# Splitting the branch weights beside the router's product, and reading their halves back from memory

## The chip, the cores and the metric

The kernel runs on one core of a Trainium2 chip. The metric is the device time of one execution in microseconds (us). Five engines matter: PE (TensorE, with PEld for its weight loads), DVE (VectorE), ACT (ScalarE), POOL (GpSimd) and SP (SyncE), which issues most transfers in one queue, in order.

## The reference

One decoder layer on 1024 tokens of width 1024, in float32. What bears on the change:

```python
u = x @ w_in                                   # projections for both mixers
y_a = dilated_mixer(a_qkv)                     # 256 wide
y_b = nsa_mixer(b_q, b_kv, b_gate, ...)        # 512 wide
merged = g_a * (y_a @ w_branch_a) + g_b * (y_b @ w_branch_b)
mix = merged @ w_out
h = layer_norm(ALPHA * x + mix, ln1_g, ln1_b)
ffn = hier_moe(h, w_coarse, ..., w_gate_up, w_down)   # router, then 2 of 32 experts
```

`w_branch_a` is 256x1024 and `w_branch_b` 512x1024: together six blocks of 128x1024.

## The kernel before, in words

Float32 products are made of three products of halves. A tile is split into a high part (a rounding copy on ACT) and a low part (the tile less its high part, on DVE or POOL): `split`, lines 120 to 125. A 128x1024 page is 512 KB.

The stages in order of time: the projections with the dilated attention; a stretch with the compression of keys and values and the router's product (up to about 475 us); the sparse attention for two groups (to about 850 us); the branch products, the gates, the output product; the experts.

PE's order is written out by hand through the attention. The projections are a stream of jobs, `stream` (line 222), of which `chunk()` gives PE six matmuls at a time between other work; their raw weights come through `wload` (line 212) and are split by `wsplit`. The other engines and SP take their order from a planner: among what is ready in its own simulated time, the instruction earliest in the program goes first. Tiles of one tag share a fixed number of pages; a page goes to the next asker when all accesses to its last tile are done. Each engine then runs its list strictly in order.

The router's product (`router`, line 750) forms w_out times the router's weights in eight steps. Each step loads one raw page `wo` of tag `t` (four pages), splits it into `woh` and `wol` in tags `th` and `tl` (two pages each, line 628), one step ahead of the product, and yields; the caller runs `for _ in wo_: chunk()` (line 818), so that projections stand between the steps. After steps 3 and 7 the sum is turned through two more pages of tag `t`, `oU` and `oT`. The compression before it uses the same three tags. `t_close()` (line 821) ends them, and the sparse attention's pages take their ground.

The six blocks of branch weights are handled in `open_branches` (line 976), called in the middle of the second group's attention, when the last projection is done and its memory is free: each block comes into one of two raw pages, ACT makes its high part, POOL its low part (`WLO` is 6), into the tag `w` of 20 pages. Right after them four blocks `y` of the branches' input go through the same two raw pages (`yload`, line 966), with the low parts on POOL too (`YLO` is 4). From that call on, what the attention issues has a raised priority in the planner. Two more blocks of `y` follow when the attention has ended, in halves, second half first; the branch products start with the second half of the tokens.

Of the kernel before, what the change touches and what calls it, by code (L numbers as in the profile page):

```python
# [9 lines left out]
FP = mybir.dt.float32  # L10
FR = mybir.dt.float32r
# [49 lines left out]
WLO = 6  # L61
# [16 lines left out]
def tile_hybrid(ctx: ExitStack, tc: tile.TileContext, x, xT, w_t, w_gate, pos_k, w1_k, w2_k, pos_v, w1_v, w2_v,  # L78
                w_a, w_b, w_out, w_oT, ln1_g, ln1_b, w_r, b_r, w_gu, w_dn, ln2_g, ln2_b, out, dbg=None):
    nc = tc.nc  # L80
    dbg = dbg or {}

    def pool(name, side, **kw):
        st = ExitStack()
        p = st.enter_context(tc.tile_pool(name=name, bufs=1, side=side, reuse_waits="tile", **kw))
        return p, st.close

    def pages(pl, tag, n):
        def f(name, dt=FP, shape=(128, 1024)):
            return pl.tile(list(shape), dt, name=name, tag=tag, bufs=n)  # L90
        return f

    def slots(pl, tag, n):

        def slot(i):
            return lambda name, dt=FP, shape=(128, 1024): pl.tile(list(shape), dt, name=name, tag=f"{tag}{i}", bufs=1)
        return [slot(i) for i in range(n)]
# [17 lines left out]
    dram = ctx.enter_context(tc.tile_pool(name="dram", bufs=1, space=DRAM))  # L115
# [4 lines left out]
    def split(raw, ph, pl, name, eng=None):  # L120
        hi = ph(name + "h", FR)
        lo = pl(name + "l", FR)
        nc.scalar.copy(hi, raw)  # L123
        (eng or nc.vector).tensor_tensor(lo, raw, hi.bitcast(FP), op=OP.subtract)  # L124
        return hi, lo
# [3 lines left out]
    def bank(tag):  # L129
        p, n, _ = ps_cur[0]  # L130
        tag = alias.get(tag, tag)
        return p.tile([128, 512], FP, name=tag, tag=tag, bufs=n[tag])
# [8 lines left out]
    def masked(pl, t, lo=None, keep=True):  # L141
        n = t.shape[1]
        m = pl("mk", FP, (128, n))
        nc.vector.tensor_scalar(m, t, 0.0, NEG, op0=OP.is_gt, op1=OP.mult)
        if lo is not None:
            m2 = pl("mk2", FP, (128, n))
            nc.vector.tensor_scalar(m2, t, lo, NEG, op0=OP.is_lt, op1=OP.mult)
            nc.vector.tensor_tensor(m, m, m2, op=OP.add)
        if keep:
            nc.vector.tensor_tensor(t, t, m, op=OP.add)  # L150
        else:
            nc.vector.tensor_copy(t, m)
# [22 lines left out]
    for k in range(8):  # L175
        r = s_pool.tile([128, 1024], FP, name=f"xr{k}")
# [67 lines left out]
    def chunk(n=1):  # L244
        for _ in range(n):
            clock[0] += 1
            next(strm, None)
            for d in [d for d in later if d[0] <= clock[0]]:
                later.remove(d)
                d[1]()  # L250
# [268 lines left out]
    def nsa_jobs(d):  # L519
        G = d["G"]  # L520
        k = (24 + 2 * G, nk_sink(d))
        v = (25 + 2 * G, v_sink(1, d["vt"], d["V"], lambda *a: nv(*a), 2))
        q = [(18 + 2 * G + p, lazy(lambda Q, p=p: q_sink(Q, d["sc"][p], 1), lambda: nq("nq", FR), 2, d["Q"][p]))
             for p in range(2)]
        return k, v, q
# [10 lines left out]
    k, v, q = nsa_jobs(N[0])  # L536
    jobs += [(22, c_sink("k")), k, (23, c_sink("v")), v, *q]
    jobs += fill[MG0:MG0 + MG1]
    k, v, q = nsa_jobs(N[1])
# [25 lines left out]
    for g in range(3):  # L565
# [3 lines left out]
        t = c_pool.tile([100, 512], FR, name=f"rw{g}")  # L569
# [58 lines left out]
    tpage, thpage, tlpage = pages(t_pool, "t", 4), pages(t_pool, "th", 2), pages(t_pool, "tl", 2)  # L628
# [121 lines left out]
    def router():  # L750
        def load(i):
            half, q = i // 4, i % 4
            r = tpage("wo", FP, (128, 2, 512))
            nc.sync.dma_start(r, w_oT[q * 256:q * 256 + 256, half * 512:half * 512 + 512].rearrange(
                "(a p) c -> p a c", p=128))
            hi, lo = thpage("woh", FR, (128, 2, 512)), tlpage("wol", FR, (128, 2, 512))
            nc.scalar.copy(hi, r)
            nc.vector.tensor_tensor(lo, r, hi.bitcast(FP), op=OP.subtract)
            return hi, lo
        ts = [load(0)]  # L760
        for i in range(8):
            if i < 7:
                ts.append(load(i + 1))
            half, q = i // 4, i % 4
            if q == 0:
                ps = bank("av")
            for j in range(2):
                for t in ts[i]:
                    nc.tensor.matmul(ps, wgd[:, 2 * q + j], t[:, j], start=q == 0 and j == 0 and t is ts[i][0],
                                     stop=q == 3 and j == 1 and t is ts[i][1])  # L770
            yield
            if q == 3:
                gT, gU = tpage("oT", FP, (64, 512)), tpage("oU", FP, (64, 512))
                nc.scalar.copy(gU, ps[64:128])
                nc.vector.tensor_tensor(gT, ps[0:64], gU, op=OP.add)
                yield
                ps = bank("pt")
                for b in range(4):
                    nc.tensor.transpose(ps[:, b * 64:b * 64 + 64], gT[:, b * 128:b * 128 + 128], ident[0:64, 0:64])
                nc.vector.tensor_copy(oW[:, 4 * half:4 * half + 4],  # L780
                                      ps[:, 0:256].rearrange("p (b c) -> p b c", b=4)[:, :, 0:36])

    wo_ = router()
    next(ck)
    chunk(3)
    for _ in range(3):
# [29 lines left out]
    masked(tpage, DW, -511.0)  # L816
    masked(tpage, MC, keep=False)
    for _ in wo_:
        chunk()
    chunk(done + 48 - clock[0])  # L820
    t_close()
# [142 lines left out]
    Y, W = [], []  # L964

    def yload(k, pgs, cut):
        hi, lo = pgs("yh", FR), pgs("yl", FR)
        for i in reversed(range(cut)):
            c = slice(i * 1024 // cut, (i + 1) * 1024 // cut)
            r = raw2("yr")  # L970
            nc.sync.dma_start(r[:, c], yad[k, :, c] if k < 2 else ybd[k - 2, :, c])
            nc.scalar.copy(hi[:, c], r[:, c])
            (nc.gpsimd if k < YLO else nc.vector).tensor_tensor(lo[:, c], r[:, c], hi[:, c].bitcast(FP), op=OP.subtract)
        Y.append((hi, lo))

    def open_branches():
        nonlocal rc_pool, rc_close, raw_pool, raw_close, raws, raw2, b_pool, b_close, bpage
        mg_close()
        w_close()
        x_close()  # L980
        rc_pool, rc_close = pool("rconst", "left")
        raw_pool, raw_close = pool("raw", "left")
        raws = slots(raw_pool, "r", NRAW)
        turns = itertools.cycle(raws)
        raw2 = lambda *a: next(turns)(*a)
        b_pool, b_close = pool("br", "left")
        bpage = pages(b_pool, "w", 20)
        for k in range(6):
            r = raw2("wab")
            nc.sync.dma_start(r, w_a[k * 128:k * 128 + 128, :] if k < 2 else w_b[(k - 2) * 128:(k - 1) * 128, :])  # L990
            W.append(split(r, bpage, bpage, "wab", nc.gpsimd if k < WLO else None))
        for k in range(4):
            yload(k, bpage, 1)

# [9 lines left out]
    for G in range(2):  # L1004
# [25 lines left out]
        for i, (n, p) in enumerate(us):  # L1030
            nxt = full(i + 2) if i + 2 < len(us) else iter(())
            grp = nsa_ta(d, n, p, P.pop(i))
            pieces = 0
            if i + 2 < len(us):
                m = us[i + 2][0]
                pieces = 2 * ((3 if m == 7 else 1 if 64 + (m + 1) * 128 <= 512 else 2) + (2 if m > 3 else 1))
            given = 0
            for gi, (tr, mul) in enumerate(grp):
                tr()
                step(mul)  # L1040
                want = pieces * (gi + 1) // len(grp)
                while given < want:
                    next(nxt, None)
                    given += 1
                    drip(0)
                drip(1)
                if G == 0 and i + 2 >= len(us):
                    chunk(2)
            for _ in nxt:
                pass  # L1050
            if G and b_pool is None and clock[0] >= end:
                open_branches()
                last_ = tc.high_priority(PRIO)
                last_.__enter__()
# [92 lines left out]
    for half in (1, 0):  # L1147
        if not half:
            mt_take(0)
        for j in range(NBR if half else 0, 8):  # L1150
# [4 lines left out]
            if (half, j) in WOJ:  # L1155
                k = WOJ.index((half, j))
# [851 lines left out]
```

## Time and profile before

| | us |
|---|---|
| median of 3 runs | 1684.24 |
| the runs | 1683.39 to 1689.32 |
| the profiled execution | 1687.2 |
| its span in the profile | 1685.3 |

The profile shows one execution: the busy time of each engine, what each waited for, and what the transfers did. Its own time is 1.9 us above its span and 3.0 us above the median of the runs.

### The profile page before, as it was taken

What the parts mean: (1) busy time and instruction counts of PE and PEld (TensorE: products, weight loads), DVE (VectorE), ACT (ScalarE), POOL (GpSimd) and SP (SyncE); (2) the same over time, 40 slices, a digit from 0 to 9 for tenths busy, and PEclk for the clock granted to TensorE, in tenths of its full rate; (3) what the DMA queues carried; (4) which work ended last, traced back from release to release, by engine and by line L of the source; (5) the groups of instructions that cost most, each with busy time, mean ns of one, the idle gap of its engine ahead of it and who ended that gap; (6) DMA issues with size and microseconds to landing.
All of it is one profiled execution on the core that took longest, in us unless ns stands there. A gap on an engine that the chain in (4) does not pass through costs nothing. (4 is left out here: it accounts for less than half of the span.)

```text
span 1685.3 us, 24695 instructions
## 1 busy us (share of the span) xinstructions
PE 1583.9 (94%) x8105; PEld 1305.3 (77%) x8105; DVE 1241.6 (74%) x2716; ACT 1113.4 (66%) x2046; POOL 469.6 (28%) x416
## 2 busy tenths in 40 slices
PE   7999999999999999999799996999999999999992
PEld 6888888777778987788678895777777777777771
DVE  5555553257867774588877797898888998989994
ACT  5566666526567785578933013778898888889882
POOL 1011113341222332323610152133431331233132
PEclk9999999999999999999999997999999999999996
DMA  7111111243420111001255767999999999999982
GB/s 267 46 38 38 39 38 63 75 110 89 148 73 31 49 34 34 25 18 52 89 206 182 297 218 255 337 342 341 368 361 356 340 346 360 366 348 358 370 281 58
DMA packets 115395, 313.87 MB, mean 186 GB/s; under 512 B 30061, under 2 KB 34285, under 8 KB 115265
## 3 DMA queue, kind: packets, MB, share of 16 engines
q1 hardware_dynamic: 101968, 287.23, 47.0%
q0 software_dynamic: 13296, 25.05, 6.0%
q8 instruction: 65, 1.06, 0.3%
q14 instruction: 66, 0.53, 0.1%
HBM read 290.04 MB, written 46.98 MB: 200 GB/s over the span
## 5 line engine op out<-in xcount | busy, mean ns | idle before, releaser
L1507 DVE TENSOR_TENSOR el<-er,eh 128x1024 fp32r<-128x1024 f32 x384 | 448.7, 1219 | 36.6 <-ACT eh L1506 34.8
L1506 ACT CAST eh<-er 128x1024 fp32r<-128x1024 f32 x384 | 391.5, 1056 | 46.8 <-PE pt L1524 33.2
L233 PE MATMUL pp<-xh,wh 128*128 128x512 f32 x672 | 271.6, 404 | 1.6 <-DVE q L288 1.6
L235 PE MATMUL pp<-xh,wl 128*128 128x512 f32 x672 | 264.7, 394 | 0.0
L234 PE MATMUL pp<-xl,wh 128*128 128x512 f32 x672 | 263.0, 391 | 0.0
L1524 PE MATMUL av<-eh,xt 128*128 128x512 f32 x512 | 196.7, 394 | 1.4 <-ACT xt L1493 1.2
L1524 PE MATMUL pt<-eh,xt 128*128 128x512 f32 x512 | 197.3, 395 | 0.0
L1550 POOL DMA_INDIRECT ybuf<-y,idx x30 | 103.3, 3444 | 172.0 <-ACT y L1549 151.0
L235 PEld LDWEIGHTS pp<-xh,wl 128*128 128x128 f32 x672 | 126.4, 188 | 29.3
L233 PEld LDWEIGHTS pp<-xh,wh 128*128 128x128 f32 x672 | 126.5, 188 | 20.8 <-DVE q L288 2.0
L1524 PE MATMUL sc<-eh,at 128*128 128x512 f32 x512 | 142.3, 399 | 0.0
L234 PEld LDWEIGHTS pp<-xl,wh 128*128 128x128 f32 x672 | 126.8, 189 | 19.2
L898 POOL TENSOR_TENSOR pw<-pw,st 128x64 f32<-128x64 f32 (+5 forms) x128 | 85.6, 698 | 185.8 <-DVE st L893 152.8
L1524 PEld LDWEIGHTS av<-eh,xt 128*128 128x128 f32 x512 | 96.8, 189 | 24.8 <-ACT xt L1493 1.6
L1524 PEld LDWEIGHTS pt<-eh,xt 128*128 128x128 f32 x512 | 96.8, 189 | 22.8
L936 DVE TENSOR_TENSOR PT<-pt,PT 128x512 fp32r<-128x512 f32 (+1 forms) x136 | 90.9, 671 | 25.8 <-ACT PT L935 24.1
L1524 PEld LDWEIGHTS sc<-eh,at 128*128 128x128 f32 x512 | 93.3, 188 | 20.7 <-ACT eh L1506 0.8
L1524 PE MATMUL av<-el,xt 128*128 128x512 f32 x256 | 106.4, 416 | 3.0 <-DVE el L1507 2.4
L1524 PE MATMUL pt<-el,xt 128*128 128x512 f32 x256 | 101.2, 396 | 0.0
L124 POOL TENSOR_TENSOR wl<-wr,wh 128x1024 fp32r<-128x1024 f32 x24 | 57.6, 2402 | 135.0 <-ACT wh L123 129.2
L935 ACT CAST PT<-pt 128x512 fp32r<-128x512 f32 (+1 forms) x136 | 76.7, 567 | 17.7 <-PE pt L928 15.9
L1401 POOL DMA_INDIRECT xg<-hbuf,idx x31 | 33.5, 1080 | 193.2 <-PE pp L1487 183.3
(447 smaller groups left out, 3600.6 us busy)
## 6 DMA issues: line engine op xcount, KB each, us to landing
er<-in_w_gu_dram SPq DMA_DIRECT2D x256, 512.0 KB
er<-in_w_dn_dram SPq DMA_DIRECT2D x128, 512.0 KB
wr<-in_w_t_dram SPq DMA_DIRECT2D x44, 512.0 KB
mgd<-mg SPq DMA_DIRECT2D x32, 256.0 KB
G<-mgd SPq DMA_DIRECT2D x32, 256.0 KB
xr<-in_xT_dram SPq DMA_DIRECT2D x8, 512.0 KB
out_dram<-in_ln_b_dram SPq DMA_DIRECT2D x8, 512.0 KB
wo<-in_w_oT_dram SPq DMA_DIRECT2D x8, 512.0 KB
```

The lines of the kernel that those rows point to most:

```text
L124: (eng or nc.vector).tensor_tensor(lo, raw, hi.bitcast(FP), op=OP.subtract)
L233: nc.tensor.matmul(ps, wh[:, kk], xh[k][:, c], start=k == 0, stop=False)
L234: nc.tensor.matmul(ps, wh[:, kk], xl[k][:, c], start=False, stop=False)
L235: nc.tensor.matmul(ps, wl[:, kk], xh[k][:, c], start=False, stop=k == 7)
L898: nc.gpsimd.tensor_tensor(t, t, st[:, 1, hi_, i:i + 1].to_broadcast([128, w]), op=OP.mult)
L935: nc.scalar.copy(t[:, 0], src)
L936: nc.vector.tensor_tensor(t[:, 1], src, t[:, 0].bitcast(FP), op=OP.subtract)
L1401: nc.gpsimd.indirect_dma_start(out=t, out_offset=None, in_=hbuf, in_offset=bass.IndirectOffsetOnAxis(ap=ids, axis=0), bounds_check=S - 1, ...
L1506: nc.scalar.copy(wh, r)
L1507: nc.vector.tensor_tensor(wl, r, wh.bitcast(FP), op=OP.subtract)
L1524: nc.tensor.matmul(pss[h], a[j == 1][:, kk], (wl if j == 2 else wh)[:, h], start=o == 0 and j == 0, stop=o == n - 1 and j == 2)
L1550: s_ = nc.gpsimd.indirect_dma_start(out=ybuf, out_offset=bass.IndirectOffsetOnAxis(ap=self.ids, axis=0), in_=y, in_offset=None, bounds_che ...
```

## The change

The six blocks are loaded and split earlier, in a generator that is stepped once after each `chunk()` of the router's loop. It uses the tags of the router: raw page `t`, high part `th`, low part `tl`, with the low part on DVE (no engine is named). Both parts are written to a new buffer in device memory, `wabd`, 12 pages of 512 KB. In `open_branches` the 12 parts are read straight into their pages; the six loads, copies and subtractions there are gone.

```diff
-    wo_ = router()
+    wabd = dram.tile([6, 2, 128, 1024], FP, name="wabd")
+
+    def branch_weights():
+        def load(k):
+            r = tpage("wab")
+            nc.sync.dma_start(r, w_a[k * 128:k * 128 + 128, :] if k < 2 else w_b[(k - 2) * 128:(k - 1) * 128, :])
+            return r
+        rs = [load(0)]
+        for k in range(6):
+            if k < 5:
+                rs.append(load(k + 1))
+            for i, t in enumerate(split(rs[k], thpage, tlpage, "wab")):
+                nc.sync.dma_start(wabd[k, i], t.bitcast(FP))
+            yield
+
+    wo_, wab_ = router(), branch_weights()
...
     for _ in wo_:
+        chunk()
+        next(wab_, None)
+    for _ in wab_:
         chunk()
...
         for k in range(6):
-            r = raw2("wab")
-            nc.sync.dma_start(r, w_a[k * 128:k * 128 + 128, :] if k < 2 else w_b[(k - 2) * 128:(k - 1) * 128, :])
-            W.append(split(r, bpage, bpage, "wab", nc.gpsimd if k < WLO else None))
+            W.append((bpage("wabh", FR), bpage("wabl", FR)))
+            for i, t in enumerate(W[k]):
+                nc.sync.dma_start(t.bitcast(FP), wabd[k, i])
```

The router yields ten times and the new generator six, so the second loop adds no `chunk()`.

## Rows read from the trace of the kernel before

**Rows 1.** The page, busy time, share of the span and instructions of each engine.
```profile
PE 1583.9 (94%) x8105; PEld 1305.3 (77%) x8105; DVE 1241.6 (74%) x2716; ACT 1113.4 (66%) x2046; POOL 469.6 (28%) x416
```

**Rows 2.** Stretches, columns: us, PE, PEld, DVE, ACT, POOL, PEclk, DMA share, GB/s.
```profile
440.00:475.00 35.00, 33.48 (x161) 26.36 (x160) 24.09 (x33) 15.59 (x24) 3.69 (x2) 1.00 0.46 150
480.00:640.00 160.00, 155.47 (x1009) 138.10 (x1010) 121.30 (x431) 124.71 (x308) 53.94 (x66) 1.00 0.12 42
795.00:850.00 55.00, 43.11 (x293) 37.81 (x292) 44.58 (x163) 49.64 (x140) 36.27 (x39) 0.94 0.29 96
860.00:910.00 50.00, 49.89 (x216) 40.55 (x217) 39.80 (x99) 15.21 (x60) 0.00 (x0) 1.00 0.46 163
```

**Rows 3.** Groups by line, ACT and then POOL, 795 to 850 us.
```profile
L123 ACT CAST wabh<-wab 128x1024 fp32r<-128x1024 f32 x6 | 6.3, 1048 | 0.0
L972 ACT CAST yh<-yr 128x1024 fp32r<-128x1024 f32 x4 | 4.2, 1050 | 0.0
...
L124 POOL TENSOR_TENSOR wabl<-wab,wabh 128x1024 fp32r<-128x1024 f32 x6 | 14.3, 2384 | 5.1 <-ACT wabh L123 5.1
```

**Rows 4.** Timeline of POOL and DVE, 800 to 812 us: start, length, engine, line.
```profile
800.94 2.39 POOL L124 TENSOR_TENSOR wabl<-wab,wabh 128x1024 fp32r<-128x1024 f32 x1 [2.39 <-ACT wabh L123]
...
802.21 1.15 DVE L890 TENSOR_SCALAR st<-st 128x6 f32<-128x6 f32 x1
...
811.73 0.17 DVE L890 TENSOR_SCALAR st<-st 128x6 f32<-128x6 f32 x1
```

**Rows 5.** Two stretches in the tail, with PEclk (columns as in rows 2).
```profile
806.00:807.00 1.00, 0.23 (x1) 0.26 (x2) 0.97 (x4) 1.00 (x3) 0.68 (x1) 1.00 0.09 29
807.00:811.00 4.00, 4.00 (x20) 3.60 (x20) 2.81 (x11) 3.03 (x12) 2.38 (x1) 0.57 0.18 40
```

**Rows 6.** Timeline around the attention's end; SP's waits, 784 to 870 us.
```profile
842.25 0.39 ACT L886 ACTIVATE pw<-pw,st 128x128 f32<-128x128 f32 x1
...
845.17 1.05 ACT L972 CAST yh<-yr 128x1024 fp32r<-128x1024 f32 x1
...
849.59 0.58 DVE L958 TENSOR_TENSOR yo<-av,T 64x128 f32<-64x128 f32 x2 [0.52 <-ACT T L949]
...
860.11 0.74 PE L1117 MATMUL sc<-yh,wabh 128*128 128x512 f32 x2 [1.17 <-ACT yh L972]
...
SPq L971 <- POOL yl L973: 9.2, 3, 3.8
```

**Rows 7.** Tile `woh` and `wol` (ns min/median/max), then PE's timeline of the router's product.
```profile
L757 ACT CAST woh<-wo x8: 1041/1050/1058, 448.0 to 468.8; 128x1024 fp32r<-128x1024 f32 x8
L758 DVE TENSOR_TENSOR wol<-wo,woh x8: 1212/1226/2196, 449.1 to 469.9; 128x1024 fp32r<-128x1024 f32 x8
...
472.37 0.39 PE L769 MATMUL av<-woh,wgd 128*128 128x512 f32 x1
...
473.07 0.40 PE L769 MATMUL av<-wol,wgd 128*128 128x512 f32 x1
```

**Rows 8.** Timeline of SP and ACT: a page's load issued, and the copy that follows.
```profile
803.35 0.33 SPq L990 DMA_DIRECT2D wab<-in_w_b_dram  x1
...
805.95 1.05 ACT L123 CAST wabh<-wab 128x1024 fp32r<-128x1024 f32 x1
...
442.84 7.84 SPq L754 DMA_DIRECT2D wo<-in_w_oT_dram  x5
...
447.98 1.05 ACT L757 CAST woh<-wo 128x1024 fp32r<-128x1024 f32 x1 [1.79 <-DMA wo<-in_w_oT_dram]
```

**Rows 9.** A page's write issued by SP, and the stretch with its last bytes.
```profile
355.90 0.32 SPq L618 DMA_DIRECT2D yad<-oT  x1
...
358.00:359.00 1.00, 1.00 (x6) 0.82 (x5) 0.63 (x1) 0.00 (x0) 1.00 (x1) 1.00 0.38 141
```

**Rows 10.** Two stretches at the kernel's start, when the queue is full.
```profile
5.00:10.00 5.00, 3.02 (x6) 1.66 (x6) 3.73 (x4) 3.68 (x4) 0.00 (x0) 1.00 1.01 369
10.00:15.00 5.00, 4.96 (x18) 3.48 (x18) 4.78 (x5) 4.07 (x5) 0.00 (x0) 1.00 1.03 419
```

## The prediction

> **What bounds the kernel now.** I first read the page for the busy shares: PE is busy 94% of the span, DVE 74%, ACT 66% [rows 1]. That average says little, so I cut the span into stretches at the places that the change touches [rows 2]. The reader should see two kinds. From 480 to 640 us PE works 97% of the time; whatever PE loses before that is lost for good. From 860 to 910 PE is full too. Between them lies a tail, 795 to 850 us, where the projections are used up and only the attention is left: PE is busy 43.1 of 55 us, ACT 49.6 and DVE 44.6. There ACT is nearest to its limit, and the six copies of the branch weights are 6.3 us of its work [rows 3]. The stretch of the router's product, 440 to 475 us, looks slack for ACT (15.6 of 35) and DVE (24.1 of 35), and the transfers are busy 46% of it, but PE is busy 33.5 of 35 [rows 2]. So the change takes work out of a stretch that ACT holds back and puts it beside a product whose pace PE sets.
>
> **The tail: what is removed.** Six ACT copies of 1.05 us, 6.3 us, and six POOL subtractions of 2.38 us, 14.3 us [rows 3]. POOL's own work is not what the attention waits for. ACT's is, but not all 6.3 us come back. Four copies of `y`, 4.2 us, stood behind the weights in the same two raw pages; with the weights gone they start earlier. Two of them, from 845.17 us on, now lie after the attention's last exponential at 842.25 us [rows 6], where ACT has time; they will move to where ACT has none. That leaves 6.3 - 2.1 = 4.2 us.
>
> A second gain sits at the end. The blocks `y` 4 and 5 wait for a raw page, which POOL's late subtractions on `y` hold: SP waits 9.2 us for them in three pieces, and PE then idles 1.17 us for the copy of `y` [rows 6]. Since the second half of these blocks depends on attention rows written long before, it can be loaded in time once the raw pages are free earlier. I count 1.3 us: the row, and a little for the step after it.
>
> DVE gains too. While POOL subtracts from 800.94 to 803.33 us, a DVE instruction on six numbers takes 1.15 us and ends with POOL's; the same instruction takes 0.17 us otherwise [rows 4]. That is 1.0 us in one place, but DVE is not the nearest limit and the four `y` subtractions come into the same stretch. I put nothing in the sum and 1.0 us in the upper end. The Trainium skill, "SBUF — State Buffer", section "Who interferes with whom", says that such a DVE instruction and a POOL instruction exclude each other for their whole length; the trace agrees here (1.15 us against 0.17). By that rule alone all six subtractions would be six chances of such a block; the sum by it would lie 1 us lower.
>
> PE's clock also fell once here: after 0.77 us of idleness in the microsecond before, four microseconds ran at 0.57 of the full clock on average, mostly at the lower of its two levels, 1.2 of 2.4 GHz [rows 5]. 4 x 0.43 = 1.7 us. A denser tail might not have that fall; I leave it to the upper end.
>
> So the tail gives 4.2 + 1.3 = 5.5 us. Upper end: 6.3 + 1.3 + 1.0 + 1.7 = 10.3 us. Lower end: nothing, if the reads collide (below).
>
> **The reads.** Twelve pages of 512 KB replace six, 6.3 MB. At the rates with a full queue, 369 to 419 GB/s [rows 10], that is 15 to 17 us from the time when the projections' pages come free, about where the tail begins. They are needed only when the branch products begin, near the attention's end, and the tail's transfers are busy 29% [rows 2]. I cost them at nothing; the cover is the 55 us of attention, and without it PE would stand for up to 17 us. What is queued behind them on SP are the small writes of the attention's output, from two pages that DVE wants back two units later.
>
> **The router: what is added.** Six loads and twelve writes by SP, six copies on ACT (1.05 us each, as for `woh`) and six subtractions on DVE (1.22) [rows 7]. ACT and DVE have room for 6.3 and 7.3 us. The pages have less. Until now eight steps turn two pages of `th`; now fourteen splits do, and a weight's page is held until its write has landed. How long that is: a lone load is followed by its copy 2.6 us after its issue; the first of five loads in a row lands after 5.1 us [rows 8]. A write was issued at 355.90 us and its last bytes moved in the slice from 358 us [rows 9], so it costs about what a load does. A page is then held 1.05 + 2.6 = 3.65 us at the low end and 1.05 + 5.1 = 6.15 at the high end. A router page is held for copy, subtraction and four matmuls. From 472.37 to 473.07 us three matmuls start [rows 7], 0.233 us each, so 0.93 for four, and 3.2 us in all.
>
> Low end: (8 x 3.2 + 6 x 3.65) / 2 = 23.8 us from the first copy at 447.98 us [rows 8] to 471.8 us, before the product's own end at 473.47. Nothing would be lost. High end: (25.6 + 36.9) / 2 = 31.3 us, to 479.2 us, 5.8 us late. The page "DMA: Bandwidth & Descriptors" of the Trainium skill, section "Anatomy of one DMA", speaks against the change: a transfer costs about 2.0 us plus its bytes over 436 GB/s, most of it the receipt of the write, worst towards device memory. That makes 3.2 us for a page, an estimate from that page; by it alone the pages would turn in 25.6 us and end at 473.5 us, no loss. The rows give 2.6 to 5.1 us, and no row isolates the receipt.
>
> The order matters as well as the sum. I walked the splits through the pages in the order in which the code asks (woh 0, 1, wabh 0, woh 2, wabh 1, woh 3, wabh 2, woh 4, wabh 3, 4, woh 5, wabh 5, woh 6, 7), with 1.05, 1.22 and 2.6 us, and 1.4 us of projection (six matmuls) between products. The first weight takes the page of woh 0 at 453.0 us, and from then on each `woh` waits for a page that it had a step ahead before. The products end at 458.6, 461.8, 466.9, 472.2, 475.4 and 477.8 us for steps 2 to 7. The largest jump is at step 5, whose raw page comes only from `oT` at about 466 us. That is 477.8 - 473.5 = 4.3 us late, with no transfer slowed by another.
>
> They will be slowed. From 442.84 us there are 8 + 6 loads, 12 writes and 2 loads of projection weights: 28 x 0.524 = 14.7 MB. At 419 and 369 GB/s that is 35 and 40 us, to 477.9 and 482.6 us: 4.4 to 9.1 us late. I take 6 us, between the walk and the middle of these, since the last weight's writes need not be done when the last product starts. Behind them on SP stand the loads of projection weights, which come a whole job ahead and can wait. On ACT and DVE the queries' copies and subtractions stand behind a split that waits for a page, and PE's two banks behind those. Upper end: 9.1 + 1.7 for one fall of the clock = 10.8 us. Lower end: 0.
>
> **Sum.** +6 - 5.5 = +0.5 us. Against the profiled execution, 1687.2 + 0.5 = 1687.7. That execution was 3.0 us above the median of the runs, so for the median I say 1684.24 + 0.5, rounded to 1685.0.
>
> **The rivals.** First, the router hides it: nothing is lost there, and the tail gives 5.5, so 1678.7 us; with the tail at its upper end 1674. For it: the low end of the page count and ACT's and DVE's room. Against it: the walk, and 14.7 MB. It decides if the pages are held under 4 us.
>
> Second, slower, by the router alone: the queue is full, ACT and DVE wait in order, PE's clock falls. At 10.8 us and a tail of 4.2 that is 1690.8; with a tail of 2 us, 1693. For it: transfers at a share of 0.46 before, with 5.2 of the 14.7 MB. Against it: PE kept its full clock through 440 to 475 us [rows 2]. It decides when a page takes 5 us or more. The same time comes out if the weights' splits slip behind the router into the attention's first units, whose pages lie on the same ground: then the change does not stay beside the product as it says.
>
> Third, the tail gives nothing, because the twelve reads delay the attention's writes or the `y` copies fill the freed time: +6 us, 1690.2.
>
> **How the numbers follow.** A case within the middle 0.50; the first rival 0.20; the second 0.17; the third 0.13. About half a per cent, 8.4 us, is what a measurement of this kernel can tell from no change, so faster is below 1675.8 and slower above 1692.7. Faster takes half of the first rival (0.10). Slower takes most of the second and a third of the third (0.18). The rest is 0.72. The range of 1677 to 1694 leaves out the first rival's upper end and jams beyond the second's worst.
>
> **What would show it.** Router: the last of its products ending near 479 to 480 us in place of 473.5; `woh` copies waiting for PE or a transfer; the stretch 440 to 475 us moving about 14 MB and PE losing some 6 us. Tail: the time from the last router product to the attention's last output, 849.59 - 473.47 = 376.1 us now [rows 6, 7], down to about 372; no idle time before the branch products near 860 us. I am wrong if the router's product ends at its old distance from its start, or more than 10 us late, or if the tail keeps its length.

## The result and the profile after

The changed kernel takes 1710.53 us (median; 1709.01 to 1711.2) beside 1686.78 us for the kernel before on the same chip: a ratio of 1.0139, 95% interval 1.0124 to 1.0153. It is slower by some 23 us; 1685.0 was predicted, with a range to 1694.

The profiled execution took 1709.01 us, its span is 1707.2. The page's first line, beside [rows 1]: PE worked 9 us more in a span that is 21.9 us longer.

```profile
PE 1592.9 (93%) x8105; PEld 1308.9 (77%) x8105; DVE 1249.6 (73%) x2722; ACT 1114.6 (65%) x2046; POOL 433.9 (25%) x410
```

To find where the 21.9 us came in, I read the same three milestones in both traces: the router's first product, its last, and the attention's last output. This view shows the instructions of one line: operation, count, shortest/median/longest in ns, first and last start.

```profile
L769 PE MATMUL av<-woh,wgd x16: 392/414/795, 454.8 to 500.4; 128*128 128x512 f32 x16
...
L769 PE MATMUL av<-wol,wgd x16: 387/406/794, 455.1 to 500.6; 128*128 128x512 f32 x16
```

The reader should see two things. The products run from 454.8 to 500.6 + 0.4 = 501.0 us, so the router's stretch is 46.2 us long; before it was 21.5 (451.9 to 473.5). And the longest matmul took 795 ns where the median is 406 to 414.

The attention's last output is a pair of instructions, which [rows 6] show as one from 849.59 us. Here the pair starts at 874.57 us, so 373.6 us follow from the router's end to there (376.1 before), and 832.6 us from there to the end (835.7 before). The sum: 24.7 us lost in the router's stretch, 2.5 and 3.1 us less behind it, and a router that started 2.9 us later. The two lengths behind the router differ by as much between single executions (374.3 and 838.3 us in a run below with the old tail), so this pair of traces alone does not give the tail's gain. The late start is no part of the change: PE's wait near 33 us, in code that both kernels share, already came 2.3 us later, and in that same run, with the same early code, the router started at 451.3.

The stretches after (columns as in rows 2): 440 to 475 us answers to the first of [rows 2], the last two to the tail and what follows it.

```profile
440.00:475.00 35.00, 27.50 (x131) 21.39 (x129) 23.70 (x31) 15.91 (x24) 4.93 (x2) 0.93 0.72 239
475.00:480.00 5.00, 0.00 (x0) 0.00 (x0) 2.54 (x3) 1.99 (x2) 0.00 (x0) 0.50 0.72 286
480.00:485.00 5.00, 4.44 (x14) 3.22 (x14) 2.03 (x3) 1.05 (x1) 0.00 (x0) 0.61 0.94 347
485.00:490.00 5.00, 0.00 (x0) 0.00 (x0) 0.00 (x0) 0.00 (x0) 0.00 (x0) 0.73 0.88 247
490.00:495.00 5.00, 2.25 (x5) 1.45 (x6) 2.36 (x2) 2.19 (x3) 0.00 (x0) 0.50 0.66 259
...
820.00:875.00 55.00, 47.60 (x321) 39.77 (x321) 47.36 (x174) 47.66 (x143) 26.57 (x37) 0.97 0.49 174
875.00:937.90 62.90, 61.32 (x264) 48.95 (x264) 46.15 (x112) 18.12 (x72) 0.00 (x0) 1.00 0.51 174
```

For ten of the 20 us from 475 on PE did nothing at all, and from 485 to 490 no engine did. The queue moved 247 to 347 GB/s there, less than the 369 to 419 of [rows 10], but it was not idle either: its share is 0.66 to 0.94, against 1.01 and 1.03 there. PE's granted clock fell with the idleness, to 0.50 (the lower of its two levels, 1.2 of 2.4 GHz); matmuls of 128x512 then took 0.63 to 0.80 us.

What PE waited for, 454 to 501 us, and then SP, 440 to 501 us (us in total, times, longest):

```profile
PE pt L779 <- DVE oT L775: 9.5, 1, 9.5
PE av L769 <- ACT woh L757: 8.5, 2, 7.3
PE av L769 <- DVE wol L758: 2.3, 3, 1.7
...
SPq L796 <- ACT wabh L123: 20.7, 6, 6.5
SPq L796 <- DVE wabl L124: 9.2, 6, 2.6
```

These three are 20.3 us. The stretch itself, after and then before (columns as in rows 2):

```profile
454.80:501.00 46.20, 25.91 (x86) 18.83 (x86) 21.14 (x23) 16.96 (x21) 2.44 (x1) 0.74 0.75 260
451.90:473.50 21.60, 20.07 (x87) 15.32 (x86) 14.00 (x17) 10.90 (x15) 2.50 (x1) 1.00 0.38 119
```

PE is idle for 20.3 us of it, where it was idle for 1.5. So 18.8 of the 24.7 us are added idle time. The other 5.8 us are the same products and projections taking longer, at a granted clock of 0.74 on average in place of 1.00. SP stood 29.9 us at line 796, the writes of the parts, waiting for the copy or the subtraction that makes them. Whatever is next in SP's line stood there too. The timeline of the worst part (start, length, engine, line, operation, tiles; in brackets the idle time before, and its releaser) shows what that was:

```profile
470.03 0.43 SPq L754 DMA_DIRECT2D wo<-in_w_oT_dram  x1
...
473.06 0.58 ACT L774 COPY oU<-av 64x512 f32<-64x512 f32 x1
476.35 1.04 ACT L757 CAST woh<-wo 128x1024 fp32r<-128x1024 f32 x1 [2.71 <-DMA wo<-in_w_oT_dram]
...
477.43 1.23 DVE L758 TENSOR_TENSOR wol<-wo,woh 128x1024 fp32r<-128x1024 f32 x1 [3.67 <-ACT woh L757]
...
478.57 1.22 DVE L124 TENSOR_TENSOR wabl<-wab,wabh 128x1024 fp32r<-128x1024 f32 x1
...
479.82 0.68 DVE L775 TENSOR_TENSOR oT<-av,oU 64x512 f32<-64x512 f32 x1
...
480.56 0.69 PE L779 MATMUL pt<-ident,oT 64*128 64x64 f32 x4 [9.49 <-DVE oT L775]
...
481.32 1.05 ACT L123 CAST wabh<-wab 128x1024 fp32r<-128x1024 f32 x1 [2.98 <-DMA wabd<-wabh]
...
484.59 0.32 SPq L796 DMA_DIRECT2D wabd<-wabl  x1
484.96 1.85 SPq L754 DMA_DIRECT2D wo<-in_w_oT_dram  x3
491.19 1.04 ACT L757 CAST woh<-wo 128x1024 fp32r<-128x1024 f32 x1 [8.82 <-DMA wo<-in_w_oT_dram]
...
492.29 0.80 PE L769 MATMUL av<-woh,wgd 128*128 128x512 f32 x1 [7.29 <-ACT woh L757]
```

Three lines wait in order here. DVE could have made `oT` soon after 473.64, when `oU` was ready; it stands behind two subtractions. The first waits for a load; the copy that the second needs stands behind the first one's copy in ACT's line. PE waits for `oT`. `wabh` waits for a page whose write is not over. Its late write holds SP's line, and the router's last three tiles are asked for at 484.96, when PE already has nothing left; it waits their whole load, 6.2 us from issue to copy. Before, such a load was asked for a step ahead.

### The profile page after: what moved, and what is told of

Same layout as the page of the kernel before. It is cut to its first block, busy times and chain, and to the rows that moved or that the text cites. A ratio compares the mean times of both kernels' runs of the same rounds, so it can differ in the third digit from the quotient of the medians.

```text
span 1707.2 us, 24741 instructions
## 1 busy us (share of the span) xinstructions
PE 1592.9 (93%) x8105; PEld 1308.9 (77%) x8105; DVE 1249.6 (73%) x2722; ACT 1114.6 (65%) x2046; POOL 433.9 (25%) x410
## 3 DMA queue, kind: packets, MB, share of 16 engines
q1 hardware_dynamic: 105424, 299.81, 48.4%
## 4 chain that ended last, share of the span: by engine, by line
PE 54%; issue 19%; DVE 9%; DMA 7%; POOL 6%; ACT 3%; SPq 0%; POOLq 0%; ACTq 0%; DVEq 0%
PE pp L233 8%; PE pp L235 8%; PE pp L234 8%; PE pt L947 3%; POOL ybuf L1569 3%; DMA xg<-hbuf,idx 3%; PE av L1543 2%; PE pt L1543 2%; PE sc L371 2%; PE sc L372 2%; PE sc L1543 2%; PE av L963 2%; PE av L964 2%; DMA wo<-in_w_oT_dram 1%; DVE el L1526 1%
## 5 line engine op out<-in xcount | busy, mean ns | idle before, releaser
L233 PEld LDWEIGHTS pp<-xh,wh 128*128 128x128 f32 x672 | 127.4, 190 | 21.2 <-DVE q L288 2.0
L1569 POOL DMA_INDIRECT ybuf<-y,idx x30 | 80.3, 2678 | 173.6 <-ACT y L1568 153.6
L1543 PEld LDWEIGHTS av<-eh,xt 128*128 128x128 f32 x512 | 96.5, 189 | 24.7 <-ACT xt L1512 1.6
```

The source lines that it names most:

```text
L233: nc.tensor.matmul(ps, wh[:, kk], xh[k][:, c], start=k == 0, stop=False)
L1543: nc.tensor.matmul(pss[h], a[j == 1][:, kk], (wl if j == 2 else wh)[:, h], start=o == 0 and j == 0, stop=o == n - 1 and j == 2)
L1569: s_ = nc.gpsimd.indirect_dma_start(out=ybuf, out_offset=bass.IndirectOffsetOnAxis(ap=self.ids, axis=0), in_=y, in_offset=None, bounds_che ...
```

## The experiments

Single executions are compared by the length of the router's stretch. Where the router's loop is untouched it was 20.8 to 22.1 us in five kernels, where the change's early part stands whole, 45.9 and 46.2. Times with an interval are paired with the kernel before on the same chip. Where an expectation speaks of 2.8 us gained on each side of the attention's last output, it is 2.5 us ahead of it and 3.1 behind it.

**The early part alone.** The end of the kernel is put back.

```diff
-            W.append((bpage("wabh", FR), bpage("wabl", FR)))
-            for i, t in enumerate(W[k]):
-                nc.sync.dma_start(t.bitcast(FP), wabd[k, i])
+            r = raw2("wab")
+            nc.sync.dma_start(r, w_a[k * 128:k * 128 + 128, :] if k < 2 else w_b[(k - 2) * 128:(k - 1) * 128, :])
+            W.append(split(r, bpage, bpage, "wab", nc.gpsimd if k < WLO else None))
```

> The early half of the change alone: the blocks are split and written beside the router's product, and the later stage loads and splits them again as before (the written copy is read by nobody). In the changed kernel the router's product takes 46.2 us from its first matmul to the end of its last (21.5 before), the stretch from there to the attention's last output 373.6 us (376.1 before), and the rest 832.6 us (835.7 before). If the early work alone makes the loss, the product takes 45 to 47 us here, the two later stretches are as before, and the whole is slower by about 25 us (ratio 1.015). Rival: the reading back takes part in the loss; then the later stretches stay short and the whole is nearer to 1.010.

Measured: 1712.7 us, ratio 1.0148 (1.0115 to 1.0181); router's stretch 45.9 us. The whole loss lies in the early part.

**Without the writes.**

```diff
+    for k in range(6):
+        nc.sync.dma_start(wabd[k, 0], w_a[k * 128:k * 128 + 128, :] if k < 2 else w_b[(k - 2) * 128:(k - 1) * 128, :])
+        nc.sync.dma_start(wabd[k, 1], zp)
...
-            for i, t in enumerate(split(rs[k], thpage, tlpage, "wab")):
-                nc.sync.dma_start(wabd[k, i], t.bitcast(FP))
+            split(rs[k], thpage, tlpage, "wab")
```

> The twelve writes beside the router are left out; the loads, copies and subtractions stay there. The later stage reads pages that were filled at the kernel's start with the unsplit blocks as high parts and zeros as low parts, so the branch products use unrounded high parts alone. Theory of the queues (a router's load stands in SP's line behind a write that waits for its data, and ACT and DVE stand in order behind splits that wait): the product takes 22 to 28 us. Theory of the pages (a page is held until its write has landed): 24 to 28 us, since a page is then free after its subtraction. Theory of the transfers' rate (14.7 MB where there were 5.2): the six loads stay, 8.4 MB, so 30 us or more.

Measured: 1703.5 us, stretch 36.5 us. The writes are worth 9.7 us; 15.0 are left without them. Only the bound of the rate's theory holds this stretch. The timeline shows what took the writes' place:

```profile
469.56 7.46 SPq L793 DMA_DIRECT2D wab<-in_w_b_dram  x2
...
477.41 2.34 SPq L760 DMA_DIRECT2D wo<-in_w_oT_dram  x3
...
484.54 1.04 ACT L763 CAST woh<-wo 128x1024 fp32r<-128x1024 f32 x1 [5.82 <-DMA wo<-in_w_oT_dram]
...
485.64 0.79 PE L775 MATMUL av<-woh,wgd 128*128 128x512 f32 x1 [3.85 <-ACT woh L763]
```

The router's three loads again come late from SP, now behind two branch loads, one of which waits for a raw page.

**High and low parts in pages of their own**, one half page each.

```diff
+    bhpage, blpage = pages(t_pool, "bh", 1), pages(t_pool, "bl", 1)
...
+            for c in (slice(0, 512), slice(512, 1024)):
+                hi, lo = bhpage("wabh", FR, (128, 512)), blpage("wabl", FR, (128, 512))
...
+                    nc.sync.dma_start(wabd[k, i, :, c], t.bitcast(FP))
```

> The high and low parts of the branch weights get one half page each of their own (128x512, so each block is split and written in two halves, the same bytes); the raw pages stay shared. Theory of the pages: the router's parts turn two pages alone as before and the product takes 22 to 27 us. Theory of the queues: the writes still stand ahead of the router's loads on SP and their waits are there still, with one page even longer ones: 35 us or more. Theory of the rate: the same bytes, 35 us or more.

Measured: 1708.99 us, stretch 46.4 us. Taking the branch parts out of the router's two high and two low pages gave nothing. But one page for each kind makes every split wait for the write of the one before, so this run does not acquit the writes.

**The writes issued by POOL.**

```diff
-                nc.sync.dma_start(wabd[k, i], t.bitcast(FP))
+                nc.gpsimd.dma_start(wabd[k, i], t.bitcast(FP))
```

> The twelve writes are issued by POOL, which has little to do there, and not by SP; pages and bytes stay. Theory of the queues, in SP's line: the router's loads come as soon as their raw page is free, and the product takes 25 to 33 us. Theory of the pages or of the rate: 42 to 48 us as in the changed kernel.

Measured: 1701.88 us, stretch 43.6 us. SP is rid of the writes, and 2.6 us come back. SP then stands 9.9 us at a branch load whose raw page the instruction of `oT` has to free, and the router's last three loads are issued at 478.49: still late. The stretch lies within the bounds of the theories of the pages and of the rate.

**A raw page of their own**, with the writes and without them.

```diff
+    wpage = pages(t_pool, "wr", 1)
...
-            r = tpage("wab")
+            r = wpage("wab")
...
             for i, t in enumerate(split(r, thpage, tlpage, "wab")):
                 nc.sync.dma_start(wabd[k, i], t.bitcast(FP))
+            if k < 5:
+                r = load(k + 1)
```

> The branch blocks come into one raw page of their own, loaded after the writes of the block before, so that the router's four raw pages hold router tiles alone; the high and low pages stay shared and the twelve writes stay on SP. The output is whole. Raw-page theory (the branch loads take two of the four raw pages, so that each of the router's tiles is asked for late and its load, 5 to 6 us, comes onto PE's path): the router's stretch falls from 46 us to 25 to 33 us and the span to 1686 to 1694 us. Rival, the writes of 6 MB fill the queues: the stretch stays at 42 us or more and the span above 1703 us. Rival, in-order ACT and DVE lines with the high and low pages: 38 to 46 us, since nothing of them changes.

> As the kernel with a raw page of its own, and the twelve writes are left out; the blocks that the end of the kernel reads are filled at the start with the unsplit weights and zeros, so that the products of the end work on weights that were never rounded into two parts. The fills delay the start of the router by about 4 us, so the stretch is compared by its own length. Left are 3 MB of loads, 12 splits through the shared high and low pages. Raw-page theory: the stretch is 22 to 26 us, near the 21.5 of the kernel before. Rival, the in-order lines of ACT and DVE: 33 us or more, as with the writes left out and shared raw pages (36.5).

Measured: 48.4 and 42.5 us. My theory that the shared raw pages make the loss fell: the stretch grew. The waits of the second kernel, 450 to 505 us, say why:

```profile
DVE wabl L124 <- ACT wabh L123: 16.3, 6, 4.5
ACT wabh L123 <- DMA wab<-in_w_b_dram: 15.3, 4, 4.7
...
PE av L775 <- ACT woh L763: 10.9, 3, 8.5
```

With one page a load starts only when the split before is over, so ACT comes to a block some 4 us too early and waits; the router's own copy is next in ACT's line. The wait for a page had become a wait for the load.

The theory of the rate, or of queues filled by the writes, kept within its bounds in each of these runs that it was set for. These are the stretches of the two kernels without writes, first with shared raw pages, then with one of its own (columns as in rows 2):

```profile
458.50:495.00 36.50, 24.92 (x86) 18.03 (x86) 20.66 (x22) 16.88 (x22) 2.45 (x1) 0.86 0.47 153
458.60:501.10 42.50, 26.00 (x87) 18.04 (x86) 20.44 (x22) 16.76 (x21) 2.49 (x1) 0.81 0.37 119
```

With almost the same loads the second stretch is 6.0 us longer and its transfers are less busy, so the rate alone does not set the length. In the change itself the transfers were busy 75% of the stretch, and how much of a load's time there is sharing, no run shows.

**The splits after the router**, between the chunks that follow.

```diff
     for _ in wo_:
         chunk()
-        next(wab_, None)
     for _ in wab_:
         chunk()
```

> The six blocks are split only once the router's loop is over, between chunks of the projections' stream; nothing is left out. Any theory in which the loss arises from standing among the router's tiles: the stretch is back at 21 to 23 us, the end keeps its gain of 2.8 us behind attention's last output, and the span goes to 1683 to 1692 us, depending on whether the first attention units wait for the splits (0 to 8 us of the 376). Rival, the volume of 9 MB costs its time wherever it is put, about 22 us at 400 GB/s: the stretch from the router's end to attention's last output grows to 390 us or more and the span stays above 1703 us.

Measured: 1702.71 us, ratio 1.0107 (1.0085 to 1.0129). The stretch is 21.2 us, but from the router's end to the attention's last output it is 394.2 us, 18.1 more than before. The first of these rows is PE at the attention's first unit, the second the splits (473 to 520 us):

```profile
PE sc L371 <- DVE st L888: 14.4, 2, 14.2
...
DVE wabl L124 <- ACT wabh L123: 10.4, 4, 3.7
```

So the neighbourhood of the router's tiles is not needed for the loss. Six splits stand in DVE's line, the last three 4.6 to 7 us apart, and whatever comes next in it makes PE wait. The rival's 390 us or more came true, with a span of 1701.3 us a little under its 1703; I had allowed 8 us. Its reason is not refuted here: from 480 to 500 us the transfers moved 290 to 412 GB/s at shares of 0.82 to 1.03, and the last splits wait for their loads.

**One block, loaded once**, so that no split waits for a load; then without the writes as well.

```diff
+    r = t_pool.tile([128, 1024], FP, name="wr")
+    nc.sync.dma_start(r, w_a[0:128, :])
     def branch_weights():
-        rs = [load(0)]
         for k in range(6):
-            if k < 5:
-                rs.append(load(k + 1))
-            for i, t in enumerate(split(rs[k], thpage, tlpage, "wab")):
+            for i, t in enumerate(split(r, thpage, tlpage, "wab")):
                 nc.sync.dma_start(wabd[k, i], t.bitcast(FP))
             yield
```

> The six splits beside the router all read one block, loaded once into a page of its own before the router's first tile, so that five of the six loads are left out and no split waits for a load (the blocks that come back are six copies of one, so the output is that of other weights). The twelve writes and the two high and two low pages are as in the change. If the uncovered latency of the loads, ahead of the router's splits in the in-order lines of ACT and DVE, makes most of the loss: the router's stretch falls from 46.2 us to 28 to 34 us, what is left over 21.5 being the writes' share (about 10 us by the kernel without writes). If the writes and the waits for pages behind them make it: 40 us or more.

> As with one resident block, and the twelve writes are left out as well; copies of unsplit blocks from memory to memory, made beside the projections, fill what the end of the kernel reads, so its products work on weights that were never split. Left of the change beside the router are six copies on ACT and six subtractions on DVE through the shared high and low pages. If the loads and writes make the loss: the stretch is 21 to 25 us. If the in-order lines themselves do (2.1 us of ACT and 2.4 to 3.4 us of DVE for each step whose products and chunk take PE 2.3 us): 28 us or more.

Measured: 37.0 and 27.7 us, both between the bounds that I had set. This takes the loss apart:

| beside the router | stretch, us | step, us |
|---|---|---|
| nothing (before) | 21.5 | |
| six copies and subtractions | 27.7 | 6.2 |
| and twelve writes | 37.0 | 9.3 |
| and the loads, through the router's raw pages (the change) | 46.2 | 9.2 |

In the other order, with the loads first (36.5 us), the loads cost 8.8 and the writes 9.7. The shares hardly depend on the order: none of the three hides behind another. These are single executions, and five untouched loops spread over 1.3 us. The last step is not the loads alone: with one block resident, the branch blocks also leave the router's four raw pages to it, and no run separates the two. What the writes do can be read in the timeline of the first of the two kernels:

```profile
474.49 1.05 ACT L757 CAST woh<-wo 128x1024 fp32r<-128x1024 f32 x1 [2.90 <-DMA wabd<-wabh]
475.59 0.77 PE L769 MATMUL av<-woh,wgd 128*128 128x512 f32 x1 [3.52 <-ACT woh L757]
...
480.02 0.32 SPq L792 DMA_DIRECT2D wabd<-wabl  x1
480.39 0.45 SPq L754 DMA_DIRECT2D wo<-in_w_oT_dram  x1
...
486.04 1.05 ACT L757 CAST woh<-wo 128x1024 fp32r<-128x1024 f32 x1 [4.50 <-DMA wo<-in_w_oT_dram]
```

A router copy waits 2.9 us for a page that a branch write still reads, and a router load leaves SP right behind a late write.

**The tail's part alone.** Nothing is split; memory is filled beside the projections.

```diff
+    def fill_block(k):
+        nc.sync.dma_start(wabd[k, 0], w_a[k * 128:k * 128 + 128, :] if k < 2 else w_b[(k - 2) * 128:(k - 1) * 128, :])
...
+                        if i in (1, 3, 5, 7, 9, 11):
+                            fill_block(i // 2)
```

> The tail's half of the change alone: nothing is split beside the router; memory is filled beside the projections by twelve copies of unsplit blocks from memory to memory, which the end reads as high and low parts, so its products work on weights that were never split. Stretch of the router 21 to 22 us. If the end gains what the prediction took: 5 to 6 us, a time of 1678 to 1681 us, ratio 0.996 to 0.997. Rival, the gain that one profiled execution showed is mostly its distance from the median: 0 to 2 us, ratio 0.999 to 1.000, and then the kernel that splits beside the projections gave up nothing there.

Measured: 1683.32 us, ratio 0.9974 (0.9961 to 0.9986), 2.4 to 6.6 us faster. The tail gives 4.4 us, less whatever the twelve copies beside the projections cost.

**The splits beside the projections**, through the projections' own pages, with the router's loop untouched.

```diff
+    def branch_weight(k):
+        r = wraw("wab")
+        nc.sync.dma_start(r, w_a[k * 128:k * 128 + 128, :] if k < 2 else w_b[(k - 2) * 128:(k - 1) * 128, :])
+        for i, t in enumerate(split(r, whi, wlo, "wab")):
+            nc.sync.dma_start(wabd[k, i], t.bitcast(FP))
...
+                        if i in BWJ:
+                            branch_weight(BWJ.index(i))
                         wsplit(i + 1)
                         wload(i + 2)
```

> The six blocks are split as jobs of the projections' stream before the router, through the projections' own raw, high and low pages, one with every other job from the second to the twelfth; the router's loop is as before; nothing is left out. If the loss is that of the place: the router's stretch is 21 to 22 us, the gain of the end stays (2.8 us behind attention's last output, and as much ahead of it), and the time is 1677 to 1684 us, faster than both by 0.2 to 0.5% and more. Rival, every split costs DMA time or ACT and DVE time where the projections have none to spare: the router's start moves from 452 to 460 us or later and the time is 1688 us or more.

Measured, with `BWJ = 1, 3, 5, 7, 9, 11`: 1685.38 us, ratio 0.9998 (0.9988 to 1.0009). The stretch is 20.8 us, but the time is that of before. PE's timeline has two waits that the kernel before does not have:

```profile
108.10 1.03 ACT L124 CAST wh<-wr 128x1024 fp32r<-128x1024 f32 x1
...
109.78 0.69 DVE L328 TENSOR_TENSOR v<-pt,v 128x512 fp32r<-128x512 f32 x1 [2.37 <-ACT v L327]
...
110.52 0.66 PE L322 MATMUL pt<-ident,vt 128*128 128x128 f32 x4 [0.53 <-DVE v L328]
...
199.09 0.66 PE L322 MATMUL pt<-ident,vt 128*128 128x128 f32 x4 [0.57 <-DVE v L328]
```

Both stand where a split follows a job of values, whose copies PE wants at once. I put this down to DVE, where a branch subtraction stood ahead. The rows show another way: DVE was idle for 2.37 us before its copy of the values and waited for ACT's, and ACT's stood behind the copy of the next projection weight, which now came after the copy of a branch block (at 103.82 us). So, the same with `BWJ = 3, 6, 7, 9, 12, 13`:

> As the kernel that splits the six blocks beside the projections, with other jobs chosen: the fourth, seventh, eighth, tenth, thirteenth and fourteenth, none of which stands behind a job of values. There PE waited twice for a value copy on DVE (0.53 and 0.57 us) that stood behind a branch subtraction. Nothing is left out. If these two waits are what the place costs beside the gain of the end (4.4 us, measured with the end's half alone): the two waits are gone, and the ratio is 0.997 to 0.999, 1.5 to 5 us faster than before. Rival, the splits there cost something that PE's rows don't show: the ratio stays at 0.9995 to 1.0005.

Measured: 1685.01 us beside 1689.03, ratio 0.9977 (0.9965 to 0.9990). The two waits are gone, and this version beats both kernels, by 1.7 to 5.9 us against the one before. The two waits were 1.1 us; that the ratio moved by 0.2%, some 3.5 us, is not explained by them, and the two intervals overlap a little.

## Why the prediction was wrong

**The step that failed** is "I take 6 us, between the walk and the middle of these". The router's term measured 24.7 us. I had worked it out twice, once from the pages and once from the bytes, and had taken the two as views of one cost, with a value between them. The runs show three costs that add: 6.2 us for the copies and subtractions, for which "ACT and DVE have room", 9.3 for the writes and 9.2 for the loads with their raw pages. The router's products ended 27.5 us late, where more than 10 was named as a sign of being wrong. PE lost 6.0 us from 440 to 475 us, the 6 that were named, but by luck: the stretch ran on to 501.

The volume was right: 14.7 MB had been counted. These rows are the transfers from 440 to 505 us (the number at the end is the median time from issue to landing):

```profile
DMA packets 5058, 14.71 MB, mean 226 GB/s; under 512 B 448, under 2 KB 448, under 8 KB 5056
...
wo<-in_w_oT_dram SPq DMA_DIRECT2D x8, 512.0 KB, 5.6
wabd<-wabh SPq DMA_DIRECT2D x6, 512.0 KB, 3.3
wabd<-wabl SPq DMA_DIRECT2D x6, 512.0 KB, 2.9
```

They moved at 226 GB/s on average, not at 369 to 419, and still at only 283 from 445 to 497 us, at a share of 0.82. By the prediction's own sum these bytes cost 4.4 to 9.1 us at the full rates, so they do not make 24.7.

The time of a write was right: 3.3 us for high parts and 2.9 us for low parts, within the 2.6 to 5.1 that I had allowed. The estimate of 3.2 us from the Trainium skill, "DMA: Bandwidth & Descriptors", section "Anatomy of one DMA", agrees with these two rows, though its fit is of transfers that GpSimd issues and these came from SP. The time of a load was not right: the walk took 2.6 us, and those of `wo` took 4.0 to 7.5, with a median of 5.6. So it does not follow from that estimate that nothing would be lost: it is short for these loads, and the order in the lines, which comes next, is not in it.

What the walk left out is the order within each engine's line. It let each split start when its page and its data were there. In the trace a tile also waits until everything ahead of it in its engine's line has had its page and data: `oT` behind two subtractions (9.5 us of PE), the router's loads behind writes that wait for a copy (7.3 us of PE), `wabh` behind the write of an earlier one (3.0 us of ACT). The prediction said that the queries' copies would stand behind a waiting split, and did not price the router's own, nor SP's. The lines also close a circle: late loads make late splits, those make late writes, and these hold SP. This would explain why taking out one link (pages, the writes' queue, the raw page) moved the stretch to 46.4, 43.6 and 48.4 us only, while each kind of work taken out moved it by 6 to 10 us; no run shows the circle by itself.

**The rivals.** The first and the third did not come about: the router lost 24.7 us, and the tail gave 4.4. The second, slower by the router alone, came about on its side, but not by its mechanism: the queue was busy but not at its full rate, a page was held some 1.05 + 3.3 = 4.35 us by the median and not 5 or more, and its price of 10.8 us was less than half. Its clause of an engine waiting in order was the right one. The clock fell as it said, after PE's waits, and cost 5.8 us in the stretch, where one fall at 1.7 us had been counted. The splits slipping "into the attention's first units" was a separate clause; in the run that moved them there they cost 18.1 us.

**The tail** was right in size: 5.5 us predicted, 4.4 measured (2.4 to 6.6) with that half alone. By place it is half right, so the size is in part luck. The first of these rows is of the kernel before, 795 to 860 us:

```profile
PE pt L928 <- DVE PT L936: 9.3, 9, 1.7
```

and these are of the change, PE from 820 to 890 us, then SP from 805 to 900 us:

```profile
PE pp L1137 <- POOL yl L992: 2.3, 2, 1.2
PE pt L947 <- DVE st L912: 1.7, 3, 0.8
PE pt L947 <- DVE PT L955: 1.6, 3, 0.8
PE sc L1136 <- ACT yh L991: 1.6, 1, 1.6
...
SPq L990 <- POOL yl L992: 12.6, 3, 4.8
```

PE's waits for the transposed weights `PT`, which ACT copies and DVE completes, fell by 7.7 us. The early part alone, with the old tail, has 9.0 us of them, and the tail's part alone 1.6, so they go with the tail. That ACT's line without the six copies does it, as the prediction had it, is likely but not shown, since the six subtractions on POOL went as well. Not all of it came back: PE's idle time in the 55 us fell from 11.9 to 7.4 us. The 1.3 us for `y` did not come. SP's wait for POOL's subtractions on `y` grew from 9.2 us [rows 6] to 12.6, and PE's waits for `y` from 1.17 to 1.6 + 2.3 us. PE from the router's last product to the last branch product took 439.8 and 438.0 us in single executions of the two kernels with the old tail, and 435.8 to 439.3 us in eleven with the new one and nothing behind the router (mean 437.2). So a part of the 4.4 us may show up by then; the rest I could not place, since the stage after it took between 765.8 and 774.5 us in single executions of code that is the same in all.

The twelve reads were hidden, as forecast: no row has PE waiting for one, with transfers busy 49% of the tail in place of 29.

## What to carry to other kernels

A stretch in which ACT, DVE and the transfers have low busy shares can still have no room: if its tiles come through in-order lines a step ahead, one foreign load, split and write per step uses up that lead, and the costs add instead of hiding behind each other. Price such an insertion by what stands next in each line (SP's first), not by busy shares, bytes or pages one at a time. Where the work can go beside a stage that keeps PE full, as here beside the projections, it is nearly free, if it keeps off the places where PE wants the same engines' results at once.

## What was not expected of the hardware

Moving the writes to POOL cost POOL 0.53 to 0.76 us for each issue, where SP's took 0.32. In the 9.5 us that PE waited for `oT` its granted clock fell, to 0.50 from 475 to 480 us, and the first matmul of 128x512 after it took 0.79 us, twice the 0.39 to 0.40 of the same instruction at a clock of 1.00. The next three took 0.63 us.
